# Shifted copies of a convolution's input by way of HBM, and a new order of each engine's work in a chunk

## Chip, cores and metric

The kernel runs on one core of a Trainium2 chip. The metric is the time of one execution on the device in microseconds (us); lower is better. Engines are called as in the profile: PE (matrix multiplies), DVE (vector engine), ACT (scalar engine), POOL (GpSimd) and SP, which only issues transfers here. "PEclk" is the clock that PE was granted, as a share of the full one.

## What is computed

A two-layer backbone over 1024 latent and 256 context tokens with 1024 channels. Layer 0 mixes tokens by a convolution module, layer 1 by windowed attention; a gated feed-forward part with a short convolution follows each. The change lies in the convolution module of layer 0 alone:

```python
def conformer_conv(h, w_pw1, b_pw1, w_dw, b_dw, ln_g, ln_b, w_pw2, b_pw2):
    u = h @ w_pw1 + b_pw1
    a, g = jnp.split(u, 2, axis=-1)
    v = a * jax.nn.sigmoid(g)
    v = dwconv(v, w_dw, b_dw)              # per channel, 31 taps, 15 tokens of padding a side
    v = jax.nn.silu(layernorm(v, ln_g, ln_b))
    return v @ w_pw2 + b_pw2

a_lat = modulate(rmsnorm(h_lat, norm1_g[i]), sh1, sc1)   # shift, scale and gate come from
y_lat = conformer_conv(a_lat, ...)                       # silu(c) @ ada_w[i] + ada_b[i] (adaLN)
y_ctx = conformer_conv(a_ctx, ...)                       # the 256 context tokens, same weights
```

## The kernel before

Channels lie on the 128 partitions, tokens along the free dimension. A matrix product is done in three passes (`mm3`, line 180): weight and input are each split into a high and a low part of float32r, and high x low, low x high and high x high are summed in PSUM. So each weight that SP loads into a `raw` buffer (two buffers of 512 KB, `load_raw`, line 107) is copied to `wh` by ACT, and the remainder goes to `wl` on DVE.

The convolution stage works on eight chunks of 128 channels (`for c in range(KC)`, line 969). For chunk c+1 the loop computes the gated unit in three token blocks (0 to 511, 512 to 1023, context): `glu_mm` on PE for gate and value, then `glu_out` (sigmoid on ACT, product on DVE) writes the block into the row buffer `v` (1325 columns with padding). In the same pass chunk c is convolved. Its 31 taps are shared out: the first 8 (16 in chunk 6, 28 in chunk 7) to PE (`pe_taps`, line 796), the next 13 (8, 0) to DVE (`dve`, line 825, one pass each over 1295 columns, accumulating into the PSUM tile `cacc`), the rest to ACT and POOL (`prod`, line 830: ACT scales into `pr`, POOL adds to `a2`). `last` (line 835) adds both sums into `ys` on DVE. `a2` and `cacc` exist once each, so chunk c+1's first product and PE taps wait for chunk c's `last`.

PE needs the input in a special form for its taps: partitions 32r to 32r+31 of a buffer hold 32 channels, shifted by r times `m` tokens (`m` = taps on PE / 4), for each of four channel groups g. `Shifted` (line 763) makes it: `load(t)` for token block t issues 16 transfers from `v` (4 shifts x 4 groups, 32 partitions each) into `vp` (one buffer, columns below `sp`) or into `vpb` (the last 512 columns). That is 48 transfers a chunk. The tap weights are packed by `pack_taps` (line 635, ACT) from a buffer that shares its place with `vp`, and spread to block-diagonal form by `tap_weights` (line 748, POOL).

Between these stand the steps of the modulation weights (adaLN) of the blocks that are needed later: `ada_steps` (line 201) gives four matmul steps on a `raw` buffer each (`ld_ada` loads them), one copy on ACT, and one step that transposes on PE and sums on DVE (`mods`).

The order on PE, ACT, DVE and POOL is the program's (`tc.manual_schedule(engines=CONV_ENGINES)`, line 15 lists these four); the order on SP isn't fixed by hand but by the planner of the framework, by when a transfer can start. Each engine executes in order, and a transfer that has to wait holds SP up.

Of the kernel before, what the change touches and what calls it, by code (L numbers as in the profile page):

```python
# [18 lines left out]
P = 128  # L19
# [10 lines left out]
TAPS = 31  # L30
# [22 lines left out]
def hybrid_dit_kernel(  # L53
# [555 lines left out]
    with ExitStack() as cs:  # L609
# [25 lines left out]
        def pack_taps(w):  # L635
            for r in range(4):
                rows = slice(32 * r, 32 * r + 32)
                for c in range(KC):
                    m = NPE[c] // 4
                    o = sum(NPE[:c]) // 4  # L640
                    nc.scalar.copy(
                        out=wpk[rows, o:o + m, :],
                        in_=w[rows, :, c * TAPS + m * r:c * TAPS + m * r + m].rearrange("p g s -> p s g"))

# [81 lines left out]
        def glu_mm(q, t, half, part=None):  # L726
# [4 lines left out]
            if part is not None:  # L731
                ops = ops[4 * part:4 * part + 4]
            mm3(q.ps[half][:, :n], ops, part is not None, part in (None, 0), part in (None, 1),
                t == 2)

        def glu_out(q, t):
            n = TOK[t][1]
            sg = cv.tile([P, 512], F32, tag="sg", name="sg", bufs=1)
            nc.scalar.activation(out=sg[:, :n], in_=q.ps[0][:, :n], func=AF.Sigmoid,
                                 bias=seg("bpw1", KC + q.c, 1), scale=1.0)  # L740
            nc.vector.scalar_tensor_tensor(out=q.v[:, VOF[t]:VOF[t] + n], in0=q.ps[1][:, :n],
                                           scalar=seg("bpw1", q.c, 1), in1=sg[:, :n],
                                           op0=ALU.add, op1=ALU.mult)

# [3 lines left out]
        def tap_weights(c):  # L748

            m = M[c]  # L750
            if m * P <= 256:
                w = cv.tile([P, 256], F32, tag="dg", name="dg", bufs=1)
            else:
                w = cv.tile([P, OW], F32, tag="pr", name="dg", bufs=2)
            w = w[:, :m * P]
            nc.gpsimd.tensor_tensor(
                out=w.rearrange("p (g m) -> p g m", m=32),
                in0=id4.unsqueeze(1).to_broadcast([P, 4 * m, 32]),
                in1=wpk[:, MO[c]:MO[c] + m, :].rearrange("p s g -> p (s g)").unsqueeze(2).to_broadcast([P, 4 * m, 32]),
                op=ALU.mult)  # L760
            return w

        class Shifted:
# [3 lines left out]
            def __init__(self, c, v):  # L767
                self.v, self.m = v, M[c]
                self.sp = OW + self.m - 1 - 512
                self.a = cv.tile([P, 4, OW - 512 + 12], F32, tag="vp", name="vp", bufs=1)  # L770
                self.b = [nt.tile([P, 512], F32, tag=("acc", "acc", "nt", "nt")[g], name="vpb",
                                  bufs=(2, 2, 3, 3)[g]) for g in range(4)]

            def copy(self, dst, c0, c1):
                for r in range(4):
                    for g in range(4):
                        x0 = self.m * r + c0
                        nc.sync.dma_start(out=dst(g)[32 * r:32 * r + 32],  # L778
                                          in_=self.v[32 * g:32 * g + 32, x0:x0 + c1 - c0])

            def load(self, t):
                e = self.sp + self.m - 1
                f = min(512, PADW + 512 - 3 * self.m)
                if t == 0:
                    self.copy(lambda g: self.a[:, g, 0:f], 0, f)
                elif t == 1:
                    self.copy(lambda g: self.a[:, g, f:e], f, e)
                else:
                    self.copy(lambda g: self.b[g], self.sp, self.sp + 512)
# [24 lines left out]
        def conv_steps(c, v, r, npe, ndve):  # L814
# [15 lines left out]
            def prod(j):  # L830
                pr = cv.tile([P, OW], F32, tag="pr", name="pr", bufs=2)
                nc.scalar.activation(out=pr, in_=v[:, j:j + OW], func=AF.Copy, scale=tap(j))  # L832
                nc.gpsimd.tensor_tensor(out=r["a2"], in0=r["a2"], in1=pr, op=ALU.add)  # L833

# [4 lines left out]

            pq = [lambda j=j: prod(j) for j in range(npe + ndve + 1, TAPS)]  # L840
            dq = [lambda j=j: dve(j) for j in range(npe, npe + ndve)]
# [42 lines left out]

        T2_FROM = 4
        with tc.manual_schedule(engines=CONV_ENGINES):
            load_next(True)
# [32 lines left out]
            glu_out(q, 0)  # L920
            vp = Shifted(0, q.v)
            vp.load(0)
            apply(1, 2, 4)
            bcast_b(2)
            pack_taps(w4)
            dgs = tap_weights(0)
            vp = Shifted(0, q.v)
            vp.load(0)
            glu_mm(q, 1, 0, 0)
# [3 lines left out]
            apply(2, 0, 4)  # L933
            apply(2, 4, 8)
            glu_mm(q, 1, 1, 0)
            glu_mm(q, 1, 0, 1)
            glu_mm(q, 1, 1, 1)
            glu_out(q, 1)
            vp.load(1)
            glu_mm(q, 2, 0)  # L940
            glu_mm(q, 2, 1)
            glu_out(q, 2)
            vp.load(2)
            load_next()
            load_next()
            ys = [make_h(t, "y") for t in range(3)]
            araw = {}
            wraw = []

            def ld_ada(c, u):  # L950
                if c < KC:
                    araw[c, u] = load_raw(adaw[0, 4 + c, :, 2 * u:2 * u + 2, :])

            def w_load():
                wraw.append(load_raw(queue[len(loaded) + len(wraw)][1]))

            def w_hi():
                wh = wpool.tile([P, 1024], F32R, tag="wh", name="wh", bufs=3)
                nc.scalar.copy(out=wh, in_=wraw[0])
                return wh  # L960

            def w_lo(wh):
                wl = wpool.tile([P, 1024], F32R, tag="wl", name="wl")
                nc.vector.tensor_sub(out=wl, in0=wraw.pop(0), in1=wh)
                loaded.append((wh, wl))

            ld_ada(0, 0)
            ld_ada(0, 1)
            for c in range(KC):
                wide_taps = M[c] * P > 256  # L970
# [5 lines left out]
                ada = ada_steps(0, 4 + c, lambda u, c=c: araw[c, u], ada_ps)  # L976
                first()
                run(pq, 1)
                if c + 1 < KC:
                    q = glu_begin(c + 1)  # L980
                    glu_mm(q, 0, 0)
                    run(ada, 1)
                    ld_ada(c, 2)
                    run(pq, 0 if wide_taps else 1)
                    glu_mm(q, 0, 1)
                    run(ada, 1)
                    ld_ada(c, 3)
                    run(taps, 4)
                    glu_out(q, 0)
# [24 lines left out]
                    run(pq, 1)  # L1014
                    w_lo(wh)
                    ld_ada(c + 1, 0)
                    wh = w_hi()
                    glu_mm(q, 2, 1)
                    run(dq, 1)
                    glu_out(q, 2)  # L1020
                    vp.load(2)
                    w_lo(wh)
                    ld_ada(c + 1, 1)
                    run(pq, 99)
                    run(dq, 99)
                else:
                    run(ada, 1)
                    ld_ada(c, 2)
                    run(ada, 1)
                    ld_ada(c, 3)  # L1030
                    run(pq, 99)
                    ymean(c - 1)
                    run(taps, 2)
                    run(ada, 2)
                    run(taps, 1)
                    run(ada, 1)
                    for i in range(4):
                        load_ada(i)
                    run(taps, 1)
                    run(dq, 99)  # L1040
# [773 lines left out]
```

## Time and profile before

| | us |
|---|---|
| median of 3 runs | 2843.6 (2837.76 to 2843.78) |
| the profiled execution | 2839.65 |
| its span, first to last instruction | 2837.9 |
| PE busy in the span | 2660.7 (94%), mean clock 0.978 |
| DVE / ACT / POOL busy | 1624.5 / 987.0 / 549.3 |
| PE in the stretch 169.5 to 214.6 (one chunk) | 39.71 of 45.1 |

The page's totals are means over stages with different limits, so the rows below are of the convolution stage, from the start of the profiled execution's span. In a timeline or the chain a row is: start, length, engine, line, what it writes and reads, how often; in brackets stands the idle time before it and what ended it. "SPq" is SP's queue of transfer issues; its lengths are issue times, not the transfer's. A line 193 matmul is one of `mm3`, line 806 a tap product, line 211 an adaLN step.

### The profile page before, as it was taken

To read this page: it belongs to the slowest core of one execution; us is meant where nothing else is said; L and a number is where in the kernel's file an instruction comes from. 1 tells how busy PE (TensorE), PEld (TensorE's weight loads), DVE (VectorE), ACT (ScalarE), POOL (GpSimd) and SP (SyncE) were. 2 spreads that over 40 slices of the span, in tenths; PEclk is the share of its full clock that TensorE was granted. 3 is DMA by queue.
4 is the path that set the end of the run, shared out by engine and by line. 5 is a ranking of instruction groups with operands and counts; after the bars stand their busy time and mean duration, and the time that the engine had idled before them with its cause. 6 is when DMAs were issued, how large, how long until landed. Compare 5 with 4: busy or idle time off the path is not lost.

```text
span 2837.9 us, 34480 instructions
## 1 busy us (share of the span) xinstructions
PE 2660.7 (94%) x13860; PEld 2166.6 (76%) x13860; DVE 1624.5 (57%) x2273; ACT 987.0 (35%) x1425; POOL 549.3 (19%) x384
## 2 busy tenths in 40 slices
PE   5688796999999999999999999899999999999997
PEld 3466572677888888888888788788878888888886
DVE  6265653555544544554455856989975455545546
ACT  6233333554222111122212524777752222222223
POOL 1356551331000000000000402556530000000003
PEclk9899998999999999999999999999999999999998
DMA  6344455431111111111111262233011111111111
GB/s 239 101 130 126 126 181 205 149 144 50 61 38 45 38 38 38 38 38 38 38 42 39 73 207 96 56 75 79 23 61 52 46 51 46 51 46 52 45 52 67
DMA packets 82736, 221.20 MB, mean 78 GB/s; under 512 B 14352, under 2 KB 25232, under 8 KB 80272
## 3 DMA queue, kind: packets, MB, share of 16 engines
q1 hardware_dynamic: 82576, 219.00, 24.0%
q8 instruction: 109, 1.79, 0.3%
q14 instruction: 51, 0.42, 0.0%
HBM read 180.89 MB, written 15.73 MB: 69 GB/s over the span
## 4 chain that ended last, share of the span: by engine, by line
PE 76%; DVE 9%; ACT 5%; SPq 3%; DMA 3%; issue 2%; POOL 1%; DVEq 0%; ACTq 0%; POOLq 0%
PE up_ps L193 37%; PE dn_ps L193 17%; PE glu_ps L193 4%; SPq L778 3%; PE wo_ps L193 2%; DMA raw<-in_adaw_dram 2%; PE pw_ps L193 2%; PE cacc L806 2%; PE pB L193 2%; PE pA L193 2%; DVE tl L178 1%; PE tp L1525 1%; PE ada_ps L211 1%; DVE mx L1503 1%; PE v_ps L193 1%
## 5 line engine op out<-in xcount | busy, mean ns | idle before, releaser
L131 DVE TENSOR_TENSOR wl<-raw,wh 128x1024 fp32r<-128x1024 f32 x167 | 207.2, 1241 | 516.2 <-issue 312.6
L193 PE MATMUL up_ps<-x_l,wh 128*128 128x512 f32 (+1 forms) x1760 | 415.1, 370 | 4.3 <-POOL x_l L322 4.3
L193 PE MATMUL up_ps<-x_h,wl 128*128 128x512 f32 (+1 forms) x1760 | 409.7, 369 | 0.2 <-ACT x_h L311 0.2
L193 PE MATMUL up_ps<-x_h,wh 128*128 128x512 f32 (+1 forms) x1760 | 408.1, 369 | 0.0
L193 PEld LDWEIGHTS up_ps<-x_l,wh 128*128 128x128 f32 x1760 | 311.9, 189 | 64.2 <-POOL x_l L322 5.8
L193 PEld LDWEIGHTS up_ps<-x_h,wh 128*128 128x128 f32 x1760 | 311.4, 189 | 55.8 <-issue 0.8
L193 PEld LDWEIGHTS up_ps<-x_h,wl 128*128 128x128 f32 x1760 | 310.6, 189 | 56.3 <-issue 0.8
L461 DVE SCALAR_TENSOR_TENSOR y<-dn_ps,mods,y 128x512 f32<-128x512 f32 (+1 forms) x400 | 270.3, 694 | 129.2 <-PE dn_ps L193 129.0
L257 POOL TENSOR_TENSOR acc<-acc,scrh 128x256 f32<-128x256 f32 (+1 forms) x36 | 37.4, 1040 | 1575.6 <-ACT scrh L256 1573.8
L416 ACT ACTIVATE c<-up_ps,pv 128x1282 f32<-128x1282 f32 (+1 forms) x88 | 115.6, 1315 | 589.3 <-PE up_ps L193 589.3
L129 ACT CAST wh<-raw 128x1024 fp32r<-128x1024 f32 x180 | 187.5, 1043 | 358.1 <-PE dn_ps L193 328.1
L193 PE MATMUL dn_ps<-gl,wh 128*128 128x512 f32 (+1 forms) x800 | 232.9, 372 | 0.7 <-DVE y L461 0.7
L193 PE MATMUL dn_ps<-gh,wl 128*128 128x512 f32 (+1 forms) x800 | 231.5, 371 | 0.0
L193 PE MATMUL dn_ps<-gh,wh 128*128 128x512 f32 (+1 forms) x800 | 231.1, 370 | 0.0
L833 POOL TENSOR_TENSOR a<-a,pr 128x1295 f32<-128x1295 f32 x62 | 189.7, 3060 | 168.7 <-ACT pr L832 166.6
L1519 POOL TENSOR_TENSOR p<-p,rd 128x640 f32<-128x640 f32 (+1 forms) x128 | 154.4, 1238 | 236.2 <-DVE rd L1517 174.1
L420 DVE SCALAR_TENSOR_TENSOR c<-up_ps,pv,c 128x1281 f32<-128x1281 f32 (+1 forms) x88 | 124.6, 1416 | 121.7 <-ACT c L416 121.7
L193 PEld LDWEIGHTS dn_ps<-gl,wh 128*128 128x128 f32 x800 | 142.7, 188 | 31.8 <-DVE y L461 6.4
L193 PEld LDWEIGHTS dn_ps<-gh,wh 128*128 128x128 f32 x800 | 145.0, 188 | 27.0
L193 PEld LDWEIGHTS dn_ps<-gh,wl 128*128 128x128 f32 x800 | 145.0, 188 | 26.9
L827 DVE SCALAR_TENSOR_TENSOR cacc<-v,pv,cacc 128x1295 f32<-128x1295 f32 x86 | 135.0, 1569 | 47.2 <-PE cacc L806 45.1
L424 DVE SCALAR_TENSOR_TENSOR c<-up_ps,pv,c 128x1281 f32<-128x1281 f32 (+1 forms) x88 | 124.5, 1416 | 2.3
(255 smaller groups left out, 4081.8 us busy)
## 6 DMA issues: line engine op xcount, KB each, us to landing
raw<-in_up_dram SPq DMA_DIRECT2D x88, 512.0 KB, 3.4
ada<-in_adaw_dram SPq DMA_DIRECT2D x11, 2048.0 KB, 8.8
raw<-in_down_dram SPq DMA_DIRECT2D x44, 512.0 KB, 3.4
raw<-in_adaw_dram SPq DMA_DIRECT2D x38, 512.0 KB, 4.6
raw<-in_pw_dram SPq DMA_DIRECT2D x32, 512.0 KB, 3.6
vp<-v SPq DMA_DIRECT2D x128, 64.0 KB, 2.0
vpb<-v SPq DMA_DIRECT2D x128, 64.0 KB, 2.0
qs<-q_dram SPq DMA_DIRECT2D x32, 256.0 KB, 5.5
```

The costliest lines, as they stand in the source:

```text
L129: nc.scalar.copy(out=wh, in_=raw)
L131: lo_engine[0].tensor_sub(out=wl, in0=raw, in1=wh)
L193: nc.tensor.matmul(ps, lhsT=w, rhs=x, start=first and n == 0, stop=last and n == len(seq) - 1)
L416: nc.scalar.activation(out=c, in_=ps[:, :W], func=AF.Identity, bias=seg("fdb", l * 2 * NJ + ab * NJ + j, 1), scale=wd[1])
L420: nc.vector.scalar_tensor_tensor(out=c[:, 1:W], in0=ps[:, 0:W - 1], scalar=wd[0], in1=c[:, 1:W], op0=ALU.mult, op1=ALU.add)
L424: nc.vector.scalar_tensor_tensor(out=c[:, 0:W - 1], in0=ps[:, 1:W], scalar=wd[2], in1=c[:, 0:W - 1], op0=ALU.mult, op1=ALU.add)
L461: nc.vector.scalar_tensor_tensor(out=h, in0=ps[:, m * n:(m + 1) * n], scalar=mod(l, 5, dc, s), in1=h, op0=ALU.mult, op1=ALU.add)
L778: nc.sync.dma_start(out=dst(g)[32 * r:32 * r + 32], in_=self.v[32 * g:32 * g + 32, x0:x0 + c1 - c0])
L806: nc.tensor.matmul(r["acc"][32 * g:32 * g + 32, o:e], lhsT=w[:, (4 * s + g) * 32:(4 * s + g + 1) * 32], rhs=vp.rows(g, s, o, e - o), start ...
L827: nc.vector.scalar_tensor_tensor(out=acc, in0=v[:, j:j + OW], scalar=tap(j), in1=acc, op0=ALU.mult, op1=ALU.add)
L833: nc.gpsimd.tensor_tensor(out=r["a2"], in0=r["a2"], in1=pr, op=ALU.add)
L1519: nc.gpsimd.tensor_tensor(out=it.p4[:, hh, :it.wid], in0=it.p4[:, hh, :it.wid], in1=rd[:, hh:hh + 1].to_broadcast([P, it.wid]), op=ALU.mult)
```

## The change

The row buffer `v` is now written to a buffer in HBM, `v_dram`, one transfer per token block, and the shifted form is read from there: one transfer per channel group brings all four shifts, by an access pattern whose dimensions are shift (4), channel (32) and token. That is 1 + 4 transfers per block and 15 per chunk. The tap weights are loaded by 4 such transfers with a shift of 0, and packed by 12 copies in place of 32. A second, unused `Shifted(0)` with its load falls away. `glu_out` is cut into its ACT step and its DVE step, so that they can stand at different places.

The order in a chunk's pass is new: on PE both block-0 products and the first two adaLN steps stand ahead of the tap products; the last adaLN step is put off into the next chunk's pass (`fin`); the first product of ACT and POOL stands behind the tap products; both weight loads stand together. Ahead of the loop, packing the taps and the loads of `Shifted` stand later, and chunk 1's weights are split by parts. Chunk 7's wide tap weights take a `v` buffer in place of a `pr` buffer.

```diff
+        def rows_of(t, pitch, first, shift, n):
+            return bass.AP(t.tensor, t.offset + first, [[shift, 4], [pitch, 32], [1, n]])
         def load_taps():
             o, n = SEG["wdw"]
             w = cv.tile([P, 4, n], F32, tag="vp", name="wdw4", bufs=1)
-            for r in range(4):
-                for g in range(4):
-                    nc.sync.dma_start(out=w[32 * r:32 * r + 32, g],
-                                      in_=par[32 * g:32 * g + 32, o:o + n])
+            for g in range(4):
+                nc.sync.dma_start(out=w[:, g],
+                                  in_=rows_of(par, NPAR, 32 * g * NPAR + o, 0, n))
 class Shifted:
+                self.d = dram.tile([P, VW], F32, name=f"v_dram{c}")
             def copy(self, dst, c0, c1):
-                for r in range(4):
-                    for g in range(4):
-                        x0 = self.m * r + c0
-                        nc.sync.dma_start(out=dst(g)[32 * r:32 * r + 32],
-                                          in_=self.v[32 * g:32 * g + 32, x0:x0 + c1 - c0])
+                for g in range(4):
+                    nc.sync.dma_start(out=dst(g),
+                                      in_=rows_of(self.d, VW, 32 * g * VW + c0, self.m, c1 - c0))
             def load(self, t):
                 e = self.sp + self.m - 1
                 f = min(512, PADW + 512 - 3 * self.m)
+                v0, v1 = ((0, PADW + 512), (PADW + 512, 2 * PADW + SEQ), (2 * PADW + SEQ, VW))[t]
+                nc.sync.dma_start(out=self.d[:, v0:v1], in_=self.v[:, v0:v1])
...
                 if c + 1 < KC:
                     q = glu_begin(c + 1)
                     glu_mm(q, 0, 0)
-                    run(ada, 1)
+                    glu_gate(q, 0)
+                    glu_mm(q, 0, 1)
+                    run(ada, 2)
                     ld_ada(c, 2)
-                    run(pq, 0 if wide_taps else 1)
-                    glu_mm(q, 0, 1)
-                    run(ada, 1)
                     ld_ada(c, 3)
                     run(taps, 4)
-                    glu_out(q, 0)
+                    glu_mul(q, 0)
+                    if fin:
+                        fin()
+                    first()
+                    run(pq, 2)
                     vp = Shifted(c + 1, q.v)
                     vp.load(0)
-                    run(pq, 1)
                     if c > 0:
                         ymean(c - 1)
                     glu_mm(q, 1, 0)
-                    run(ada, 1)
+                    run(pq, 1)
+                    glu_gate(q, 1)
+                    run(ada, 2)
+                    w_load()
                     w_load()
                     run(dq, 3)
-                    run(pq, 2)
-                    run(ada, 1)
-                    w_load()
+                    run(pq, 1)
                     glu_mm(q, 1, 1)
                     run(ada, 1)
                     run(dq, 3)
+                    glu_mul(q, 1)
+                    vp.load(1)
                     run(pq, 1)
-                    glu_out(q, 1)
-                    vp.load(1)
                     if M[c + 1] * P <= 256:
                         dgs = tap_weights(c + 1)
                     wh = w_hi()
                     glu_mm(q, 2, 0)
-                    run(ada, 1)
-                    run(dq, 2)
-                    run(pq, 1)
+                    run(dq, 1)
                     w_lo(wh)
                     ld_ada(c + 1, 0)
+                    run(pq, 1)
+                    glu_gate(q, 2)
                     wh = w_hi()
                     glu_mm(q, 2, 1)
                     run(dq, 1)
-                    glu_out(q, 2)
+                    glu_mul(q, 2)
                     vp.load(2)
                     w_lo(wh)
                     ld_ada(c + 1, 1)
                     run(pq, 99)
                     run(dq, 99)
+                    fin = ada.pop()
```

## Rows read from the trace of the kernel before

**Rows 1.** Chain of waits, 0 to 820 us: start us, us, what.

```profile
125.22 4.36 PE cacc L806 x56
...
169.55 3.90 PE cacc L806 x51
174.34 5.68 PE glu_ps L193 x24
180.02 1.00 PE ada_ps L211 x8
181.02 8.55 PE glu_ps L193 x48
...
209.22 4.29 DMA raw<-in_adaw_dram
...
400.19 8.27 PE cacc L806 x115
...
450.16 10.22 PE cacc L806 x102
...
461.25 6.20 PE cacc L806 x109
```

**Rows 2.** Timeline of SP's issues in chunk 1's pass: start, us, queue, line, what.

```profile
198.86 10.24 SPq L778 DMA_DIRECT2D vpb<-v  x16
209.22 5.75 SPq L109 DMA_DIRECT2D raw<-in_adaw_dram  x3
```

**Rows 3.** Busy time of each engine in chunk 1's pass.

```profile
core 0: us, PE busy (x) PEld busy (x) DVE busy (x) ACT busy (x) POOL busy (x), PEclk, DMA share, GB/s
169.50:214.60 45.10, 39.71 (x240) 30.22 (x234) 29.47 (x24) 17.55 (x16) 28.96 (x14) 0.92 0.46 130
```

**Rows 4.** Timeline of PE, 190 to 210 us.

```profile
192.71 2.00 PE L193 MATMUL glu_ps<-xl,wh 128*128 128x512 f32 x8
...
203.65 1.92 PE L211 MATMUL ada_ps<-raw,c 128*32 128x512 f32 x4 [2.87 <-DMA raw<-in_adaw_dram]
205.50 3.78 PE L193 MATMUL glu_ps<-xl,wh 128*128 128x512 f32 x8
```

**Rows 5.** Timeline of DVE, 170 to 200 us.

```profile
173.96 9.61 DVE L827 SCALAR_TENSOR_TENSOR cacc<-v,pv,cacc 128x1295 f32<-128x1295 f32 x6 [4.38 <-PE cacc L806]
...
198.19 0.48 DVE L741 SCALAR_TENSOR_TENSOR v<-glu_ps,pv,sg 128x256 f32<-128x256 f32 x1
```

**Rows 6.** Timeline of SP's issues, 0 to 130 and 380 to 480 us.

```profile
48.27 0.84 SPq L109 DMA_DIRECT2D raw<-in_pw_dram  x2
67.00 32.97 SPq L778 DMA_DIRECT2D vp<-v  x48
100.08 10.05 SPq L778 DMA_DIRECT2D vpb<-v  x16
...
400.61 0.43 SPq L862 DMA_DIRECT2D ada<-in_adaw_dram  x1
405.56 14.81 SPq L778 DMA_DIRECT2D vp<-v  x16
```

**Rows 7.** Timeline of PE, 28 to 128 us.

```profile
114.60 1.92 PE L211 MATMUL ada_ps<-raw,c 128*32 128x512 f32 x4 [22.69 <-DMA raw<-in_adaw_dram]
```

**Rows 8.** List of transfers: what, count, KB each, median us from issue to landing.

```profile
vp<-v SPq DMA_DIRECT2D x128, 64.0 KB, 2.0
...
q_dram<-rh SPq DMA_DIRECT2D x16, 256.0 KB, 2.0
```

**Rows 9.** Busy time by stretch, 6 to 13 us; last two: DMA share, GB/s.

```profile
6.00:13.00 7.00, 0.00 (x0) 0.00 (x0) 0.49 (x1) 1.67 (x4) 0.00 (x0) 1.00 1.05 417
```

**Rows 10.** Timeline of POOL, 160 to 216 us.

```profile
170.14 12.18 POOL L833 TENSOR_TENSOR a<-a,pr 128x1295 f32<-128x1295 f32 x4
```

**Rows 11.** Timeline of ACT, 28 to 128 us.

```profile
62.95 3.98 ACT L641 COPY wpk<-wdw 32x8 f32<-32x8 f32 x32
...
77.46 0.60 ACT L698 ACTIVATE h<-h,mods,amul 128x256 f32<-128x256 f32 x1
```

More of the change, by code (lines that the diff above doesn't have):

```diff
@@ L628, in load_taps @@
             w = cv.tile([P, 4, n], F32, tag="vp", name="wdw4", bufs=1)
-            for r in range(4):
-                for g in range(4):
-                    nc.sync.dma_start(out=w[32 * r:32 * r + 32, g],
-                                      in_=par[32 * g:32 * g + 32, o:o + n])
+            for g in range(4):
+                nc.sync.dma_start(out=w[:, g],
+                                  in_=rows_of(par, NPAR, 32 * g * NPAR + o, 0, n))
             return w
         def pack_taps(w):
-            for r in range(4):
[L637 to L640, printed above, removed]
+            c0 = 0
+            while c0 < KC:
+                m = NPE[c0] // 4
+                n = sum(x == NPE[c0] for x in NPE[c0:])
+                o = sum(NPE[:c0]) // 4
+                for r in range(4):
+                    rows = slice(32 * r, 32 * r + 32)
+                    src = w[rows].rearrange("p g (c t) -> p c t g", t=TAPS)
                     nc.scalar.copy(
-                        out=wpk[rows, o:o + m, :],
-                        in_=w[rows, :, c * TAPS + m * r:c * TAPS + m * r + m].rearrange("p g s -> p s g"))
+                        out=wpk[rows, o:o + n * m, :].rearrange("p (c s) g -> p c s g", s=m),
+                        in_=src[:, c0:c0 + n, m * r:m * r + m, :])
+                c0 += n
         def ada_src(b, ks):
@@ L734, in glu_mm, with glu_gate, glu_mul @@
                 t == 2)
-        def glu_out(q, t):
[L737 to L743, printed above, removed]
+        def glu_gate(q, t):
+            n = TOK[t][1]
+            q.sg = cv.tile([P, 512], F32, tag="sg", name="sg", bufs=1)
+            nc.scalar.activation(out=q.sg[:, :n], in_=q.ps[0][:, :n], func=AF.Sigmoid,
+                                 bias=seg("bpw1", KC + q.c, 1), scale=1.0)
+        def glu_mul(q, t):
+            n = TOK[t][1]
+            nc.vector.scalar_tensor_tensor(out=q.v[:, VOF[t]:VOF[t] + n], in0=q.ps[1][:, :n],
+                                           scalar=seg("bpw1", q.c, 1), in1=q.sg[:, :n],
+                                           op0=ALU.add, op1=ALU.mult)
+        def glu_out(q, t):
+            glu_gate(q, t)
+            glu_mul(q, t)
         M = [n // 4 for n in NPE]
@@ L832, in prod @@
                 nc.scalar.activation(out=pr, in_=v[:, j:j + OW], func=AF.Copy, scale=tap(j))
-                nc.gpsimd.tensor_tensor(out=r["a2"], in0=r["a2"], in1=pr, op=ALU.add)
+                return lambda: nc.gpsimd.tensor_tensor(out=r["a2"], in0=r["a2"], in1=pr, op=ALU.add)
             def last():
@@ L838, in last @@
                                             in1=r["a2"][:, OOF[t]:OOF[t] + n], op=ALU.add)
-            pq = [lambda j=j: prod(j) for j in range(npe + ndve + 1, TAPS)]
+            pq = [lambda j=j: prod(j)() for j in range(npe + ndve + 1, TAPS)]
             dq = [lambda j=j: dve(j) for j in range(npe, npe + ndve)]
@@ L885, in hybrid_dit_kernel, with ld_ada, w_load, w_hi @@
         T2_FROM = 4
+        araw = {}
+        wraw = []
+        def ld_ada(c, u):
+            if c < KC:
+                araw[c, u] = load_raw(adaw[0, 4 + c, :, 2 * u:2 * u + 2, :])
+        def w_load():
+            wraw.append(load_raw(queue[len(loaded) + len(wraw)][1]))
+        def w_hi():
+            wh = wpool.tile([P, 1024], F32R, tag="wh", name="wh", bufs=3)
+            nc.scalar.copy(out=wh, in_=wraw[0])
+            return wh
+        def w_lo(wh):
+            wl = wpool.tile([P, 1024], F32R, tag="wl", name="wl")
+            nc.vector.tensor_sub(out=wl, in0=wraw.pop(0), in1=wh)
+            loaded.append((wh, wl))
         with tc.manual_schedule(engines=CONV_ENGINES):
@@ L934, in hybrid_dit_kernel @@
             apply(2, 4, 8)
+            pack_taps(w4)
+            dgs = tap_weights(0)
             glu_mm(q, 1, 1, 0)
@@ L937, in hybrid_dit_kernel @@
             glu_mm(q, 1, 1, 1)
+            w_load()
+            w_load()
+            vp = Shifted(0, q.v)
+            vp.load(0)
             glu_out(q, 1)
             vp.load(1)
+            wh = w_hi()
             glu_mm(q, 2, 0)
+            w_lo(wh)
             glu_mm(q, 2, 1)
@@ L943, in hybrid_dit_kernel @@
             vp.load(2)
-            load_next()
-            load_next()
+            w_lo(w_hi())
             ys = [make_h(t, "y") for t in range(3)]
[L947 to L965, printed above, removed]
             ld_ada(0, 0)
             ld_ada(0, 1)
+            fin = None
             for c in range(KC):
@@ L1025, in hybrid_dit_kernel @@
                     run(dq, 99)
+                    fin = ada.pop()
                 else:
-                    run(ada, 1)
+                    run(ada, 2)
                     ld_ada(c, 2)
-                    run(ada, 1)
                     ld_ada(c, 3)
+                    fin()
+                    first()
                     run(pq, 99)
```

19 lines of the change are left out of this document (5 added, 14 removed).

## The prediction, on record before the changed kernel ran

> **What bounds the kernel now.** I read the chain of waits first, since it says which engine each stretch of the convolution stage (some 50 to 468 us) waits for. A chunk's period shows in the starts of PE's tap products (line 806): 125.2, 169.6, ... 400.2, 450.2 [rows 1], that is 44.3 us, then 230.6 / 5 = 46.1 us each, then 50.0. Ahead of the products stands a load of `raw` of 4.3 us, and it was issued only when SP had got through the copies of the chunk's last token block: 16 copies take SP 10.24 us, 0.64 us each, the adaLN load follows at 209.22 and lands at 213.5 [rows 1, 2]. PE is in order, so products and everything behind them wait. The table by stretch shows that PE isn't the limit yet: 39.7 us busy of 45.1, at a mean clock of 0.92 [rows 3]; after an idle wait of 2.87 us eight matmuls took 3.78 us where the same eight took 2.00 before it [rows 4], so a wait costs some 1.8 us of clock besides. Chunk 1's products end at 169.55 + 3.90 = 173.45, and PE's last gated-unit matmul of the chunk ends at 192.71, where the next chunk's first starts [rows 1, 4]: 19.3 us. I call that end E. The part of v that the last copies need is written by DVE from 198.19 on [rows 5], 5.5 us after E, since modulation sums, taps and a weight split stand before it.
>
> The stage also starts late for SP's sake: SP issues 64 copies from 67.0 to 110.1 (one group of 16 twice), and PE, idle for 22.7 us, gets its adaLN data at 114.6 [rows 6, 7].
>
> **The edits, one by one.** All durations are from one profiled execution of 2839.65 us (span 2837.9); the median of the three runs, 2843.6, is 4 us above it, which I add at the end.
>
> *Copies.* Per chunk 48 issues x 0.64 = 31 us of SP go. In their place come 3 writes to HBM and 12 reads, at the same 0.64 at most 10 us, so SP has time to spare. But reads wait for their write: the nearest row, a 256 KB write of q, lands in 2.0 us [rows 8]. SP stands still meanwhile, with raw loads queued behind it.
>
> *How fast a read is.* Each reads 4 shifts x 32 rows, 256 KB, and the source's outermost dimension counts 4. No row has that. All 16 engines together moved 417 GB/s at full share [rows 9], 26.1 each. If a read is cut over 16 engines, a piece of 4 reads (a and c, for the first and last token block, 1.05 MB; b between them, 0.56 MB) takes 2.5, 1.3 and 2.5 us; if over four, 104 GB/s, it takes 10.1, 5.4 and 10.1. These are the two ends. I take four: the transfers of the trace are cut along dimensions of 32 or 128 parts, multiples of 16, and this one offers four. The old copies don't decide it (32 rows each, landing in 2.0 us [rows 8]).
>
> The Trainium skill (DMA: Bandwidth & Descriptors, "Why a DMA increments its semaphore by 16 and not by 1") states that a DMA takes the largest number of engines up to 16 that divides the count of the slowest dimension on both sides; by that rule it is four and the sum below holds, by sixteen it would be the first rival's. It speaks against this change, and no row of the trace shows it.
>
> *A chunk with four engines.* DVE's product for block 1 ends at E - 5.0 (PE then has 2 x 2.87 us of block-2 matmuls left [rows 1], DVE needs 0.7). Write b has landed 2.5 us later, its issue included; b's reads start about 1 us after that, take 5.4 and some gaps, and end at E + 4.5. A raw load of 512 KB (1.3 us at 417 GB/s) follows, to E + 5.8. Block 2's v is now ready at E + 1.2, as the modulation sums move to the next chunk and five taps go behind it; its write queues on the same four engines and lands near E + 7.9. Reads c start at E + 9, end at E + 19.1 and have landed at E + 20. PE meanwhile has 2 x 5.68 = 11.4 us of block-0 matmuls, 1.0 of adaLN [rows 1] and the first two of the four tap parts, half of 4.36: it is at E + 14.6, idles 5.4 us, and the last two parts take 2.2 + 1.8 of clock, to E + 24. So the period is 24 + 19.3 = 43.3 us against 46.1.
>
> This needs the second adaLN load to be issued while SP would wait for write c. SP's order isn't written out by hand (line 15 lists the four other engines). In the trace two loads of chunk 1's weights that stand behind the copies in the program were issued ahead of them, at 48.27, and a block of layer 1's adaLN weights, written in chunk 7, came at 400.61, ahead of chunk 7's first copies at 405.56 [rows 6]. I take it that this goes on.
>
> *Other engines.* Thirteen taps at 1.60 [rows 5] and some 9 us of the rest make 30 for DVE; nine additions at 3.05 [rows 10] and the tap weights make 28 for GpSimd; both fit under 43.3. The split of the gate, the pairing of weight loads and the moved first product I cost at nothing, hidden by PE's matmuls; at a period of 36 GpSimd would keep some 2 us of that cover (its nine additions follow ACT's two first steps), and if it is gone those chunks are bound by GpSimd at up to 38.
>
> *Start of the stage.* Packing the taps takes ACT 3.98 us for 32 copies [rows 11]; 12 longer ones take 1.5 to 4, say 2, now behind the last normalization, which ends at 78.06 before and comes 4 us sooner. Reads a, which need that buffer, start at about 77 and end at 87; b, whose write lands behind a, ends at 95; a write, two raw loads and c end near 109 and have landed at 111. Products end at 111 + 2.2 + 1.8 and 2 of queue gaps = 117 instead of 125.22 + 4.36 = 129.6: -12.6 us.
>
> *Sum.* End of chunk 6's products: 117 + 5 x 43.3 + 45.5 (their second half is 2.2 longer) = 379.0 against 400.19 + 8.27 = 408.5. Chunk 7: 19.3 to E; reads c land at E + 20, and 5 later with two 2 MB loads ahead (5.0 us each at 417 GB/s, one beside other work); then half of its products, 7.7 + 1.8: 379.0 + 19.3 + 34.5 = 432.8 against 461.25 + 6.20 = 467.45 [rows 1]. That is -35 us: 2805 for a profiled execution, 2809 for the median. Behind the stage nothing is edited.
>
> **Rivals.** *All 16 engines.* Reads c land before E + 9, PE waits for none and bounds the chunk: 19.3 + 11.4 + 1.0 + 4.4 = 36.1. Products of chunk 0 end at 102 (27 us of SP's queue gone), of chunk 6 at 102 + 5 x 36.1 + 40.5 = 323, of chunk 7 at 323 + 19.3 + 28 = 370: -97, so 2747. For it: no row shows a transfer on fewer; against it: the count of four.
>
> *The adaLN load stays behind reads c* (slower). If SP keeps the program's order at that place, the second adaLN half lands at E + 21.7 and PE waits there, ahead of all four tap parts: 21.7 + 0.5 + 4.4 + 1.8 + 19.3 = 47.7 a chunk, 1.6 above now. Chunk 6's products end at 117 + 5 x 47.7 + 52.1 = 407.6, chunk 7's, all behind that wait, 19.3 + 21.7 + 5 + 17 = 63 later at 470.6: +3, so 2847. Reads b and c stand in this loop, so each 10% on a row (8 ns of 79 for 2 KB) adds 1.6 us a chunk, 13 in all: at 95 ns it is 2873. It is slower than before from about 81 ns a row. For it: in chunk 1 the load came behind all 16 copies [rows 2]. Against it: the loads that went ahead [rows 6].
>
> **How the numbers follow.** Four engines with the load ahead: 0.55; sixteen: 0.17; load behind: 0.28, of which 0.16 slower, 0.10 within the bound and 0.02 faster. In the first case rows of 75 to 95 ns give 2802 to 2838, so 0.53 of it is faster and 0.01 each for the rest. The bound is 0.2% or 5.7 us, about what a measurement of this kernel can tell from no change. Faster: 0.53 + 0.17 + 0.02 = 0.72; same 0.11; slower 0.17. The range of 2765 to 2868 leaves out the sixteen engines (0.17) and little of the rest.
>
> **What would show it.** As forecast: reads into `vp` and `vpb` that take over 10 us a piece, starts of line 806 some 43 us apart, and a wait between its second and third part. Second rival: a wait at an adaLN matmul instead, starts 47 us apart. First rival: starts 36 us apart, PE's clock at 0.99 or more. The term for the start is wrong if chunk 0's products don't end between 113 and 121, and the whole account is if DVE or GpSimd, not a transfer, ends PE's waits.

## The result, and the profile after

| | before | after |
|---|---|---|
| median of all runs, us | 2841.3 (4 runs) | 2855.5 (4 runs, 2853.7 to 2858.7) |
| the profiled execution, us | 2839.65 | 2854.50 |
| its span, us | 2837.9 | 2852.7 |
| PE busy in the span, us; mean clock | 2660.7; 0.978 | 2669.1; 0.973 |

The ratio after to before is 1.0052, with a 95% interval of 1.0035 to 1.0070: the change costs some 14 us. The forecast was a gain of 35 us (2809). 2855 lies inside the stated range, but it is a slowdown, to which 0.17 had been given. One execution of all those reported below, of e8, took 4396 us at a granted PE clock of 0.557; the ratios leave it out.

First the page of the changed kernel, for a first hint: the shares of the chain that ended last, by engine and by line.

```profile
PE 75%; DMA 9%; DVE 8%; ACT 5%; issue 2%; SPq 1%; POOL 1%; DVEq 0%; ACTq 0%; POOLq 0%
PE up_ps L193 37%; PE dn_ps L193 17%; DMA vpb<-v_dram 3%; DMA v_dram<-v 3%; PE glu_ps L193 3%; PE wo_ps L193 2%; PE pw_ps L193 2%; PE pB L193 2%; PE pA L193 2%; PE cacc L822 2%; PE tp L1545 1%; DVE tl L178 1%; PE v_ps L193 1%; SPq L792 1%; DVE mx L1523 1%
```

Transfers now hold 9% of the chain, and the two names are the two halves of the change: the write to HBM and the read from it. SP's issues, which the change was to relieve, are down to 1%; they were 3% before, with DMA at 3%. So one queue went and another came.

Where in the stage? The ends of PE's tap products (line 806 before [rows 1], 822 after), from the timeline of PE, chunk by chunk, and beside them the forecast:

| products' end of | before | forecast | after | after minus forecast |
|---|---|---|---|---|
| chunk 0 | 129.6 | 117 | 120.2 | +3.2 |
| five periods (chunks 1 to 5) | 230.9 (46.2 each) | 216.5 (43.3) | 235.6 (47.1) | +19.1 |
| chunk 6 | 48.4 | 45.5 | 53.3 | +7.8 |
| chunk 7 | 58.6 | 53.8 | 76.1 | +22.3 |
| end of chunk 7 | 467.5 | 432.8 | 485.2 | +52.4 |

The start is 9.4 us sooner than before, the six middle chunks give that back (4.7 + 4.9), and chunk 7 alone loses 17.5. At the stage's end the changed kernel is 17.7 us late, at the end of the span 14.8.

One chunk close up, the one of [rows 2 to 5], with E at 185.00. SP's issues in the changed kernel (start, length of the issue, line, what):

```profile
183.11 2.22 SPq L792 DMA_DIRECT2D vp<-v_dram  x4
185.44 0.46 SPq L109 DMA_DIRECT2D raw<-in_adaw_dram  x1
186.00 2.01 SPq L799 DMA_DIRECT2D v_dram<-v  x1
188.10 0.38 SPq L109 DMA_DIRECT2D raw<-in_adaw_dram  x1
194.78 2.26 SPq L792 DMA_DIRECT2D vpb<-v_dram  x4
197.15 2.73 SPq L109 DMA_DIRECT2D raw<-in_adaw_dram  x2
```

and PE over the same time:

```profile
185.00 2.00 PE L193 MATMUL glu_ps<-xl,wh 128*128 128x512 f32 x8
...
195.99 1.06 PE L211 MATMUL ada_ps<-raw,c 128*32 128x512 f32 x8
198.52 2.84 PE L822 MATMUL cacc<-vp,dg 128*32 128x512 f32 x32 [1.47 <-issue]
201.16 0.57 PE L822 MATMUL cacc<-vpb,dg 128*32 128x240 f32 x2
203.42 0.59 PE L822 MATMUL cacc<-vpb,dg 128*32 128x240 f32 x2 [1.70 <-DMA vpb<-v_dram]
206.92 1.01 PE L822 MATMUL cacc<-vpb,dg 128*32 128x240 f32 x2 [2.90 <-DMA vpb<-v_dram]
209.56 3.62 PE L822 MATMUL cacc<-vpb,dg 128*32 128x240 f32 x26 [1.63 <-DMA vpb<-v_dram]
```

Block 2's write is issued at 186.00, and the reads that wait for it at 194.78: 8.8 us for a write of 135.5 KB. It stands behind reads b (183.11), and the packets show on how many engines: of the write's 128 rows 96 start from 189.1 to 190.1, and the other 32, a share of four engines in 16, only from 193.0 to 194.2, after the last row of reads b has started (192.5). The last read of c lets PE go on at 209.56, 14.8 us after the first was issued. PE gets the channel groups of the block one by one, and idles ahead of the last three. The second adaLN load (188.10) did go ahead of reads c, so the adaLN wait of [rows 4] is gone. The table of waits says it for four chunks, first of before (129.6 to 314.7 us), then of after (120.2 to 308.8 us); columns: who waits for what, us in total, times, longest.

```profile
PE ada_ps L211 <- DMA raw<-in_adaw_dram: 20.4, 8, 4.9
PE glu_ps L193 <- DVE wl L964: 8.3, 4, 2.3
```

```profile
PE cacc L822 <- DMA vpb<-v_dram: 24.5, 12, 3.1
PE cacc L822 <- issue: 5.3, 4, 1.8
```

28.7 us of waits before, 29.8 after: the wait for adaLN weights behind SP's issue queue has become a wait for the shifted reads themselves. (The "issue" of the second table is a wait for DVE: in chunks 1 to 6 the tap products start 0.1 us after DVE's `last` has read `cacc`, in this chunk after 198.42.) The clock stays low with it, 0.93 in chunk 1's pass (0.92 in [rows 3]):

```profile
165.50:213.20 47.70, 40.00 (x235) 27.70 (x236) 27.18 (x23) 17.31 (x16) 28.34 (x13) 0.93 0.47 137
```

Chunk 7 is another story. SP, then PE in the changed kernel:

```profile
419.38 0.33 SPq L878 DMA_DIRECT2D ada<-in_adaw_dram  x1
423.90 0.33 SPq L799 DMA_DIRECT2D v_dram<-v  x1
...
438.16 2.55 SPq L792 DMA_DIRECT2D vp<-v_dram  x4
440.81 5.63 SPq L792 DMA_DIRECT2D vpb<-v_dram  x4
446.54 3.19 SPq L109 DMA_DIRECT2D raw<-in_adaw_dram  x2
```

```profile
439.51 1.92 PE L211 MATMUL ada_ps<-raw,c 128*32 128x512 f32 x4 [10.78 <-DMA raw<-in_adaw_dram]
463.99 1.92 PE L211 MATMUL ada_ps<-raw,c 128*32 128x512 f32 x4 [22.56 <-DMA raw<-in_adaw_dram]
...
467.76 10.32 PE L822 MATMUL cacc<-vp,dg 128*32 128x512 f32 x109
```

Write b, issued at 423.90 right behind a load of 2 MB (419.38) and reads a, is waited for until 438.16: 96 of its 128 rows start from 429.6 to 430.7, the other 32 from 435.9 to 437.5; reads b and c go out together; and the second adaLN load stands behind both (446.54), where in the earlier chunks it went ahead. PE idles 22.6 us for it, with all tap products queued behind.

How many engines a read uses can be counted. The page gives the packets under 512 B, of before and of after:

```profile
DMA packets 82736, 221.20 MB, mean 78 GB/s; under 512 B 14352, under 2 KB 25232, under 8 KB 80272
```

```profile
DMA packets 79421, 225.53 MB, mean 79 GB/s; under 512 B 8480, under 2 KB 20384, under 8 KB 76960
```

If every transfer leaves one small packet on each engine that it uses, and copies and writes use all 16, the 416 copies that fell away (48 x 8, 16 unused, 16 for the tap weights) take 16 x 416 = 6656 with them, 24 writes bring 384, and 100 reads bring 100 k. The count went down by 5872, so k is 4, to the packet.

### The profile page after: what moved, and what is told of

Same layout as the page of the kernel before. It is cut to its first block, busy times and chain, and to the rows that moved or that the text cites. A ratio compares the mean times of both kernels' runs of the same rounds, so it can differ in the third digit from the quotient of the medians.

```text
span 2852.7 us, 34110 instructions
## 1 busy us (share of the span) xinstructions
PE 2669.1 (94%) x13860; PEld 2155.7 (76%) x13860; DVE 1609.8 (56%) x2273; ACT 984.0 (34%) x1405; POOL 549.7 (19%) x384
## 2 busy tenths in 40 slices
DMA packets 79421, 225.53 MB, mean 79 GB/s; under 512 B 8480, under 2 KB 20384, under 8 KB 76960
## 4 chain that ended last, share of the span: by engine, by line
PE 75%; DMA 9%; DVE 8%; ACT 5%; issue 2%; SPq 1%; POOL 1%; DVEq 0%; ACTq 0%; POOLq 0%
PE up_ps L193 37%; PE dn_ps L193 17%; DMA vpb<-v_dram 3%; DMA v_dram<-v 3%; PE glu_ps L193 3%; PE wo_ps L193 2%; PE pw_ps L193 2%; PE pB L193 2%; PE pA L193 2%; PE cacc L822 2%; PE tp L1545 1%; DVE tl L178 1%; PE v_ps L193 1%; SPq L792 1%; DVE mx L1523 1%
## 5 line engine op out<-in xcount | busy, mean ns | idle before, releaser
L843 DVE SCALAR_TENSOR_TENSOR cacc<-v,pv,cacc 128x1295 f32<-128x1295 f32 x86 | 134.9, 1569 | 24.4 <-PE cacc L822 22.3
```

The source lines that it names most:

```text
L843: nc.vector.scalar_tensor_tensor(out=acc, in0=v[:, j:j + OW], scalar=tap(j), in1=acc, op0=ALU.mult, op1=ALU.add)
```

## The experiments

The theory, F: a read whose outermost dimension counts 4 uses four engines, and the queue on these four is what PE waits for. The rivals: the detour through HBM itself is too slow (H), or the new order is at fault (O). All runs are compared with the kernel before, run on the same chip beside them.

| kernel | median, us | ratio to before, 95% interval | period, chunks 1 to 5, us | chunk 7, us |
|---|---|---|---|---|
| e1_outer32 | 2759.3 | 0.9718 [0.9702, 0.9733] | 39.1 | 54.5 |
| e2_order_alone | 2842.7 | 1.0005 [0.9994, 1.0017] | 47.5 | 60.4 |
| e3_transfers_alone | 2845.6 | 1.0018 [1.0005, 1.0030] | 47.6 | 69.5 |
| e4_reads32 | 2793.1 | 0.9832 [0.9816, 0.9847] | 39.4 | 58.3 |
| e5_c_reads32 | 2823.5 | 0.9934 [0.9909, 0.9960] | 45.0 | 68.1 |
| e6_old_order32 | 2764.4 | 0.9726 [0.9701, 0.9750] | 40.8 | 47.0 |
| e7_last_sbuf | 2843.4 | 1.0009 [0.9998, 1.0019] | 47.7 | 62.1 |
| e8_taps_first | 2749.2 | 0.9676 [0.9653, 0.9699] | 38.7 | 43.7 |
| e9_no_ada_loads | 2820.1 | 0.9920 [0.9892, 0.9949] | 44.3 | 59.4 |
| e10_two_shifts | 3052.3 | 1.0742 [1.0717, 1.0767] | 73.1 | 92.7 |

**e1_outer32: the same bytes, 32 outermost.** Channel and shift change places, in the access pattern and on the partitions (4 x channel + shift in place of 32 x shift + channel); the tap weights are loaded and packed to match.

```diff
-[[shift, 4], [pitch, 32], [1, n]]
+[[pitch, 32], [shift, 4], [1, n]]
 ...
-in_=ident.rearrange("p (r m) -> p m r", m=32)
+in_=ident.rearrange("p (m r) -> p m r", r=4)
 ...
```

> The changed kernel with channel and shift swapped in the read's access pattern: its outermost dimension counts 32 (channels), the shift of 4 lies inside it, and partition 4p+r holds channel p at shift r (the tap weights and the small identity are laid out to match). Number, size and order of the transfers stay. Theory F (the reads ran on four of the 16 engines and those four queues set the chunk): reads of the last block land within 9 us of their write's end instead of 14.7, PE bounds the chunk, period 36 to 39 us, total 2745 to 2775 us. Rival H (the detour by HBM, a write that must land before the reads, sets it, on however many engines): 2850 to 2860. Rival O (the new order costs the time): over 2841.

2759.3 us, 96 below the changed kernel: F holds, H falls. The reads c of one chunk (185 to 213 us) in SP's timeline, and PE's waits from 96.2 to 253.2 us:

```profile
196.84 0.33 SPq L799 DMA_DIRECT2D v_dram<-v  x1
...
199.43 2.85 SPq L792 DMA_DIRECT2D vpb<-v_dram  x4
```

```profile
PE cacc L822 <- issue: 8.9, 4, 2.2
```

The write is waited for 2.6 us instead of 8.8, and PE waits for no transfer any more. What is left is DVE: ahead of its tap products PE idles 2.2 us until `last` has read `cacc`, and that puts the period at 39.1, just past the 39 expected. In the same chunk:

```profile
206.85 1.62 DVE L853 TENSOR_TENSOR y<-cacc,a 128x512 f32<-128x512 f32 x3
208.57 2.84 PE L822 MATMUL cacc<-vp,dg 128*32 128x512 f32 x32 [2.22 <-issue]
```

In the packets of the trace, the 512 rows of 2 KB of one block 2 start within 4.0 us (201.7 to 205.7), where the changed kernel's took 12.8 (196.2 to 209.0); the median row took 84 ns here and 86 there. The median row costs the same; what differs is the number of engines that carry the rows. Twelve reads of tap weights for four, 16 small packets a read in place of 4, and 1024 short rows of tap weights add 176 + 1152 + 1024 = 2352 to the changed kernel's 8480, and the page says 10832.

**e2_order_alone: the order without the transfers.** The 48 copies from `v` and the tap loads of before, everything else as in the changed kernel.

```diff
-                nc.sync.dma_start(out=self.d[:, v0:v1], in_=self.v[:, v0:v1])
 ...
-                    nc.sync.dma_start(out=dst(g), in_=rows_of(self.d, ...))
+                    for r in range(4):
+                        nc.sync.dma_start(out=dst(g)[32 * r:32 * r + 32],
+                                          in_=self.v[32 * g:32 * g + 32, x0:x0 + c1 - c0])
```

> The new order of all engines with the 48 copies from SBUF of the kernel before (and its loads of the tap weights). F: the order itself gains, since SP's 10 us of issues for the last block end before PE reaches the tap products at E + 14: period 37 to 41, 2765 to 2800 us. O: the order costs, 2850 us or more.

2842.7 us, no difference from before: both expectations missed. SP in one chunk (E at 187.26), and PE where it waits:

```profile
182.56 11.20 SPq L794 DMA_DIRECT2D vp<-v  x16
...
194.63 10.01 SPq L794 DMA_DIRECT2D vpb<-v  x16
204.74 1.03 SPq L109 DMA_DIRECT2D raw<-in_adaw_dram  x2
```

```profile
208.86 1.07 PE L211 MATMUL ada_ps<-raw,c 128*32 128x512 f32 x2 [8.94 <-DMA raw<-in_adaw_dram]
```

Block 2's value is ready sooner, but its 16 issues stand behind the 16 of block 1, and the adaLN load behind both. An earlier product is worth nothing while the queue behind it is 21 us long.

**e3_transfers_alone: the transfers without the order.** The order of before, with the reads and writes of the changed kernel, and without the unused first `Shifted`.

> The order of the kernel before with the new transfers (one write and four reads a block, unused first group dropped). F: with only 5.7 us of PE work ahead of the first adaLN step instead of 11.4 the wait for the last block's piece grows; period 48 to 52, 2860 to 2890 us, slower than the changed kernel. H expects the same sign. O: below 2841.

2845.6 us, 14 below the least expected. Without the new order the transfers cost less, so that order adds some 10 us to their loss and doesn't make up for any of it (the two intervals just miss each other). PE's waits of 114.5 to 305.7 us:

```profile
PE cacc L811 <- DMA vpb<-v_dram: 13.0, 8, 2.2
PE ada_ps L211 <- DMA raw<-in_adaw_dram: 11.0, 4, 3.8
```

Both kinds of wait are there, the one of before and the one of after.

**e4_reads32: the detour kept, the reads cut small.** Each read from HBM is cut into four of 32 partitions, 51 transfers a chunk, more than the 48 of before.

```diff
+                for r in range(4):
                     for g in range(4):
+                        x0 = self.m * r + c0
-                        nc.sync.dma_start(out=dst(g), in_=rows_of(self.d, ...))
+                        nc.sync.dma_start(out=dst(g)[32 * r:32 * r + 32],
+                                          in_=self.d[32 * g:32 * g + 32, x0:x0 + c1 - c0])
```

> The changed kernel with each read cut into four of 32 partitions, so 16 reads a block still from HBM, 51 transfers a chunk. F: each read spreads over 16 engines again; SP needs some 7 us for 16 issues, the piece lands about 10 us after its write: period 37 to 41, 2755 to 2800 us. H: as the changed kernel, 2850 to 2860. If the number of transfers were what counts: 2841 or more.

2793.1 us: F's range holds, and with partitions laid out as in the changed kernel. HBM isn't the cause. The page's count of packets:

```profile
DMA packets 85184, 225.58 MB, mean 81 GB/s; under 512 B 14240, under 2 KB 26144, under 8 KB 82720
```

Its 14240 small packets are 8480 + 384 x 16 - 96 x 4, again to the packet. It is 34 us slower than e1; its first products end at 118.4, e1's at 96.2, so 22 of these 34 are lost at the start of the stage, where SP issues its first 48 reads in 24.1 us, 12 in 7.4 in e1.

**e5_c_reads32: only block 2's reads cut small.** The edit of e4, for `vpb` alone.

> The changed kernel, but block 2's piece alone is read by 16 transfers of 32 partitions; the pieces of blocks 0 and 1, and the tap weights, still go by reads of four engines. If the reads of block 2 on four engines (14.7 us in chunk 1) are what PE idles for, they land at about E + 13, ahead of PE's tap products: periods of 38 to 41 us, 2775 to 2810 us in all. If the queue ahead of them is what counts (write c, 8.8 us behind reads b on the same four engines), the write still lands at E + 9.8, periods are 42 to 44 us and the total is 2815 to 2835. If the detour through HBM as such is the cause, 2850 to 2860.

2823.5 us: the total is that of the case in the middle, the queue ahead of reads c; the period, 45.0, is 1 us above it. SP in one chunk, and PE's waits of 113.4 to 291.2 us:

```profile
179.71 2.23 SPq L792 DMA_DIRECT2D vp<-v_dram  x4
...
182.62 0.38 SPq L799 DMA_DIRECT2D v_dram<-v  x1
...
190.94 7.29 SPq L808 DMA_DIRECT2D vpb<-v_dram  x16
```

```profile
PE glu_ps L193 <- ACT sg L746: 13.9, 4, 5.6
PE cacc L826 <- DMA vpb<-v_dram: 3.6, 4, 2.0
```

The write still takes 8.3 us behind reads b. And a wait shows that I had not thought of: PE waits for ACT's gate (line 746), which stands behind a `wh` copy on ACT, and that copy waits for a raw load of conv weights, 8.4 us in this chunk. That load was issued at 166.60, behind reads a at 161.55, and ACT could go on at 177.73, 11 us later; the median of such a load in the list of before is 3.6. So the reads on four engines most likely hold up this load too, as they do the write.

**e6_old_order32: the order of before with all 16 engines.** e3 with the access pattern of e1, and with e1's loading and packing of the tap weights.

> The order of before with the 15 transfers a chunk in the form with 32 channels outermost (all 16 engines); with e1, e2, e3 and before it shows what the order is worth once no queue stands behind block 2's product. DVE's product of block 2 comes at E + 5.5 in this order, write and reads take some 5 us, so the second adaLN load lands near E + 12.5, when PE has done block 0 and the first adaLN step: if the copies and the reads alone were the limit, the order is worth little here and the time is 2760 to 2790. If the new order is needed for the gain (DVE's late product holding back the load of the adaLN weights), periods stay at 42 to 45 us and the time is 2800 to 2830.

2764.4 us: the expected 2760 to 2790. With e1, e2, e3 and before, the four cells are complete:

| transfers | order of before | new order |
|---|---|---|
| 48 copies | 2841 | 2843 |
| 15, four engines | 2846 | 2855 |
| 15, 16 engines | 2764 | 2759 |

The number of engines is worth 81 to 96 us in a column; the order costs 10 us on four engines, and on 16 its gain of 5 isn't clear of the noise (the intervals of e1 and e6 overlap). The profiled executions show why it is small: the new order gains 1.7 us in each of chunks 1 to 5 (39.1 against 40.8) and loses 7.5 in chunk 7 (54.5 against 47.0).

**e7_last_sbuf: chunk 7 by the old copies.** The changed kernel, with `copy` and `load` of chunk 7 alone as before.

> The changed kernel, with chunk 7's pieces alone by the 48 copies from SBUF of before. If chunk 7's 76.1 us (before: 58.5) come from its wide reads on four engines, which hold up the raw load behind them, its products end some 15 to 18 us sooner and the time is 2836 to 2842. If they come from the 2 MB loads that were moved ahead of them or from the order, it stays at 2850 to 2858.

2843.4 us, 1.4 above the expected range: chunk 7 takes 62.1 us in place of 76.1, so 14.0 of the 17.5 us that it lost go with its detour by four-engine reads. What the rest is stays open.

**e8_taps_first: a better version.** e1, and in chunk 7 the first half of the tap products ahead of the adaLN steps for whose loads PE idled in e1:

```diff
-                    run(ada, 2)
-                    ld_ada(c, 2)
-                    ld_ada(c, 3)
                     fin()
 ...
                     run(taps, 2)
+                    run(ada, 2)
+                    ld_ada(c, 2)
+                    ld_ada(c, 3)
+                    run(taps, 2)
                     run(ada, 3)
 ...
-                    run(taps, 2)
```

> The form with 32 channels outermost (e1), and in chunk 7 half of the tap products ahead of the adaLN steps, for whose loads PE idled 3.8 + 8.7 us there. If the loads of adaLN weights behind the reads bound the end of that chunk, 5 to 11 us go: 2748 to 2755 us. If the tap products only change places with a wait for their own reads, it stays at 2757 to 2763.

2749.2 us, 3.2% below before and as expected. PE's waits at the end of the stage, first of e1 (336 to 391 us), then of e8 (335.8 to 379.5):

```profile
PE ada_ps L211 <- DMA raw<-in_adaw_dram: 12.6, 2, 8.7
```

```profile
PE ymean L862 <- DVE y L853: 4.4, 1, 4.4
```

Chunk 7 takes 43.7 us in place of 54.5.

**e9_no_ada_loads: how much of it is sharing.**

```diff
+            vt[c] = q.v
 ...
-                araw[c, u] = load_raw(adaw[0, 4 + c, :, 2 * u:2 * u + 2, :])
+                if c == KC - 1:
+                    araw[c, u] = load_raw(adaw[0, 4 + c, :, 2 * u:2 * u + 2, :])
+                else:
+                    araw[c, u] = vt[c][:, 0:1024]
```

> The changed kernel without the loads of the adaLN weights of chunks 0 to 6 (four raw loads of 512 KB a chunk; PE's adaLN steps read v in their place, so their sums are not the reference's). It asks how much of the lost time is other loads sharing the four engines of the reads. If the reads of block 2, 14.7 us in chunk 1, are slowed by the raw loads behind and ahead of them, they come down to 128 rows an engine x 86 ns = 11 us and a start of 1 to 2, so 12 to 13 us, the periods to 43 to 45 us and the time to 2825 to 2840. If sharing plays no part and the read's own rate is what was mis-sized, the periods stay at 47 to 48 and the time at 2848 to 2857.

2820.1 us, 5 below the expected range; periods of 44.3, inside it. SP in one chunk (E at 181.94), and PE at the end of the reads:

```profile
184.46 0.33 SPq L800 DMA_DIRECT2D v_dram<-v  x1
...
190.94 2.43 SPq L793 DMA_DIRECT2D vpb<-v_dram  x4
```

```profile
204.43 1.93 PE L823 MATMUL cacc<-vpb,dg 128*32 128x240 f32 x16 [2.07 <-DMA vpb<-v_dram]
```

The write is waited for 6.5 us in place of 8.8, the reads take 13.5 in place of 14.8. In the packets, the mean of the 512 rows of 2 KB goes from 104 to 92 ns, with the median at 84 to 86 in both. So without the adaLN loads on the same engines 2.8 of the 3.8 us go by which the period was above the forecast. The kernel also frees SP and the `raw` buffers of these loads, so sharing isn't shown alone; the mean row is what speaks for it. Chunk 7, whose own adaLN loads are still there, comes down by 16.7: its second load now goes out at 422.70, ahead of reads c at 430.19.

**e10_two_shifts: two engines.** Each read cut into two of 2 shifts x 32 channels, the same bytes and rows.

```diff
                 for g in range(4):
+                    for r in (0, 2):
-                    nc.sync.dma_start(out=dst(g), in_=rows_of(self.d, ..., 4 shifts))
+                        nc.sync.dma_start(out=dst(g)[32 * r:32 * r + 64],
+                                          in_=rows_of(self.d, ... + self.m * r, ..., 2 shifts))
```

> The changed kernel, with each read of the shifted form cut into two of 2 shifts x 32 channels: 24 reads and 3 writes a chunk, the same bytes in the same rows, outermost dimension 2 in place of 4. If the outermost count sets how many engines a transfer uses, and always the same first ones, each piece goes over two engines and takes twice as long: in a chunk, what is left of reads b behind E and all of reads c come on top, some 5 + 13 = 18 us, so periods near 65 us and 2960 to 3020 us in all. If the two halves use different engines, or the number of engines isn't what counts, it stays at 2845 to 2870.

3052.3 us, above the expected 2960 to 3020; the mechanism is the one expected, its price too low, at 73.1 us a chunk in place of 65. SP's issues of reads c in one chunk, and PE's waits from 140 to 400 us:

```profile
264.00 12.50 SPq L793 DMA_DIRECT2D vpb<-v_dram  x8
```

```profile
PE cacc L824 <- DMA vpb<-v_dram: 51.1, 12, 5.5
PE glu_ps L193 <- ACT sg L746: 35.0, 4, 9.6
```

Eight issues take SP 12.5 us, where four take 2.3 in the changed kernel. The expectation had counted the reads alone; PE also waits 8.8 us a chunk for ACT's gate, which stands behind a load of conv weights as in e5. That both halves use the same two engines shows in the write of block 2: 112 of its 128 rows start from 258.3 to 259.3, the other 16 from 262.8 to 263.4. The page counts 8480 small packets, the same as with half as many reads on four engines: 192 x 2 = 96 x 4. With 16, 4 and 2 engines (e1, the changed kernel, e10) the period is 39, 47 and 73 us.

The Trainium skill (DMA: Bandwidth & Descriptors, "Why a DMA increments its semaphore by 16 and not by 1") has a transfer use the largest number of engines up to 16 that divides the count of the slowest dimension on both sides. Counts of 32, 4 and 2 gave 16, 4 and 2 here, by the packets and by the time.

## Why the prediction was wrong

*Four engines: right.* It was the branch that was chosen against the one of 16, on the count of 4 alone. The packet counts and e1, e4 and e10 show it.

*Start of the stage: right within 3.2 us.* 120.2 against 117, inside the 113 to 121 that were named. SP's old queue of 43 us is gone, but reads a were issued at 76.9, and block 1's write behind them held SP until 91.9.

*The adaLN load ahead of reads c: right in the chunks 1 to 6, wrong in 7.* At 188.10 it goes ahead. In chunk 7 it goes out behind reads b and c (446.54), as in the second rival; PE waits 22.6 us. The prediction had taken one order of SP for all chunks.

*Write c at E + 7.9: E + 9.8.* The queueing of the write behind reads b was seen; the raw load between them was counted at 1.3 us, its time on all engines. Where the adaLN loads are left out (e9), the write is waited for 6.5 us in place of 8.8, and reads c go out at E + 9.0.

*Reads c, E + 9 to E + 20: E + 9.8 to E + 24.6. This is the step that failed in the chunks 1 to 6.* 10.1 us of transfer had come from [rows 9], where all engines are at full share, as 26.1 GB/s each, 79 ns a row. The row's median is 86 ns, and the mean 104. The likely reason is that two raw loads are issued right behind the reads (197.15) and have their shares on the same four engines; their rows of 4 KB start from 200 us on, among those of the reads. The prediction itself had the sensitivity, given for its second rival: 1.6 us a chunk for each 10% on a row, so 104 for 79 ns would have made 43.3 + 5.1 = 48.4; it is 47.1. That range of rows, 75 to 95 ns, stopped short, because it was thought of as the row's own price, not as a price under sharing. e9 takes away the adaLN loads and comes to 44.3, with a mean row of 92 ns.

*Chunk 7: 53.8 forecast, 76.1 measured, the largest single miss.* The step that failed here is the order of SP, and write b with it. In e9 SP's order is the forecast one again and 16.7 of the 22.3 us are gone; in e7, with the old copies, 14.0. Write b, issued 4.5 us behind a 2 MB load, was waited for 14.3 us, where the sum had 2.5. Its first rows start 5.7 us after its issue, and the last quarter of them, those on the engines of the reads, another 6.3 us later. No run separates SP's order from this wait.

*Chunk 6: +7.8.* 3.8 of it is the period's. The second half of the products was counted with 2.2 us more; e1, where PE waits for no transfer, has 44.5 - 39.1 = 5.4 for it. That is 3.2 more; the last 0.8 us stay open.

*The order.* That the early product of block 2 carries the gain was the reason of the whole sum. e2 and e6 show that it doesn't: nothing with a long queue behind it, and with a short one 5 us that aren't clear of the noise.

*The other rivals.* The one with 16 engines was sized at 2747 and a period of 36.1; e1 gives 2759 and 39.1, e8 2749. Its mechanism was PE as the limit, with GpSimd as the next; in e1 it is DVE that ends PE's waits, 2.2 us a chunk. The prediction had DVE at 30 us of work and asked only whether that fits in the period. The slow rival was sized at 2847 with 47.7 a chunk: the time and the period came close by luck, since in seven chunks of eight the reason was another.

Taken together: 12.6 of the 34.7 us were the start, and 9.4 of them came. The other 22 stood on a loop of reads b, write c and reads c with a margin of some 3 us a chunk (43.3 against 46.2; chunk 7 4.8), and every omission in that loop made it longer.

## What to carry to other kernels

Fewer transfers aren't faster transfers: before folding copies into one access pattern, look at which dimension ends up outermost, and lay the partitions out so that a multiple of 16 stands there; here 32 in place of 4 alone is worth 96 us. When a transfer uses few engines, price what is queued behind it too, writes and loads of other streams among them, since each has a share on the busy engines. Reordering the work ahead of a long queue gained nothing here, and ahead of a short one little.

## What the runs showed of the hardware beyond that

- The packets under 512 B on the page count engines: in before, after, e1, e4 and e10 they come out to the packet with one per transfer and engine (and one for each row that is itself shorter).
- A 135.5 KB write that uses all engines was waited for 8.8 us behind reads on four of them, 2.6 us in e1.
- SP's issue isn't of constant length: a read with 4 outermost takes 0.57 us, one with 2 outermost 1.56 in a full queue, a copy of 32 partitions from SBUF 0.64 and one from HBM 0.46.
- DVE's split of a weight (`wl`, 128 x 1024 elements) has a median of 3.05 us in e1 (134.7 to 213.1 us) and of 1.22 in the changed kernel (120 to 213). The difference goes with POOL: in the twelve traces, up to 520 us, all 106 splits that start while no POOL instruction runs take 1.21 to 1.23 us; the other 140 take up to 3.96. In e1 the time falls on DVE's path to `last`, so it is part of what PE waits for there.
